# The mixer's output projection by seven products per pair of output tiles, part of them beside the delta rule

## The chip, the core and the metric

The kernel runs on one core of one Trainium2 chip. The metric is device time in microseconds (us); the figure that is compared is the median of several executions, and one further execution was profiled. TensorE (PE) multiplies, VectorE (DVE) and ScalarE (ACT) split operands and move results, GpSimd (POOL) does a few elementwise steps and issues the transfers that add into their destination, SyncE (SP) issues most loads. Transfers of all queues run on the same 16 DMA engines.

## The reference, cut to what matters

One layer of an encoder trunk on 512 tokens of width 2048. The change concerns the end of the mixer and one piece of the cross-attention:

```python
o = gated_delta_rule(q, k, v, g, beta)              # 8 heads x 128 channels, chunks in sequence
y_gdn = rmsnorm(o, out_gain) * silu(z)               # 1024 channels, "heads"
y_sc  = b_gate * causal_dwconv(c_gate * h, conv_w)   # 1024 channels, "convolution"
x = x + concatenate([y_gdn, y_sc], -1) @ w_mix_out   # 2048 x 2048: the output projection
...
v = (mem_n @ w_v)                                    # 256 memory tokens, 4 heads x 512
o = einsum('bhsm,bmhd->bshd', softmax(s), v)
x = x + o @ w_o                                      # w_o = w_xo
```

The kernel never forms `o @ w_o`: it multiplies each head's values by that head's rows of `w_xo` once (the *fold*) and applies the probabilities to the product.

## The kernel before

Everything is fp32, and accuracy is kept by splitting an operand into a high part, rounded to the matmul's format, and a low part, the difference: one ACT cast and one DVE subtraction. In the *three-product form* (`mm3`, L154) a weight block costs three matmuls of 512 columns per 128 channels: high weights by high and by low activations, low weights by high ones. In the *two-product form* (`mm2s`, L168) the activations of half the tokens (256) lie with their high and low parts side by side in one 512-column operand `xo`, so a block costs a matmul of 512 columns with the high weights and one of 256 columns with the low ones.

The stages, in order of time:

- *Values and fold* (to about 193 us). The values of the four heads; then 16 steps (L669 on), a head's quarter of the output columns each: two blocks of `w_xo`, 24 matmuls of 512 columns, results `psmo` scaled into `mo` and stored in `mo_d`. Beside it the operands of the input projection are prepared (`up_prepare`).
- *Input projection* (to 738 us): 28 pairs of output tiles, each by Strassen's scheme in the form with seven products of half size instead of eight, in the two-product form. Sums of weight blocks come partly from DMAs that add into their destination (L544, L550, issued by POOL), partly from DVE.
- *Keys, and queries folded into keys* (738 to 969 us). From here on the delta rule is woven in: generators issue its small steps, and `tick`, called after each planned piece of PE work with that piece's cost, decides when the next step's instructions are issued.
- *Output projection, first half* (from 969 us): `out_row` (L1076) for 16 output tiles, the eight convolution blocks each, 24 matmuls in the three-product form; tile plus `x` goes to `xp_d` in HBM. It is what PE does while the delta rule waits between its steps. *Second half* (to 1177 us): the heads' results `y_d` are loaded (L1074), split, and 16 tiles of 24 matmuls follow; `xp_d` is added, the row stored in `x1_d`, squared for the norm, and split into the operands of the next stage.
- *Scores* (`pss`, 1177 to 1268 us): four sweeps of 96 matmuls, each over the 16 tiles of `x1` against `wk_d`. Then the attention's output and the feed-forward network.

PE's order is the program's in stretches marked `manual_schedule`, and a list scheduler's elsewhere; each engine then runs its list strictly in order, and an instruction waits for the data it needs. The lists of SP and POOL are in order too, so a DMA issue that waits holds back all behind it. Weight blocks are staged in five buffers (`wst`), sums in four (`us`).

## Time and profile before

| | us |
|---|---|
| three runs | 2658.38, 2660.89, 2663.46 (median 2660.89) |
| the profiled execution | 2657.3 (its span, first to last instruction: 2655.5) |
| output projection in the profile, `psx` L156 to L158 | 968.9 to 1177.0 |
| the fold, `psmo` | 99.9 to 193.0 |
| scores, `pss` L1187 to L1189 | 1177.2 to 1267.7 |
| PE busy over the span | 2641.0 |
| granted TensorE clock | 0.999 |

Rows of stretches name the window and then, for each engine, busy time with the number of instructions, the granted clock, the mean busy share of the 16 DMA engines (packets can overlap, so it may pass 1) and the rate of what they moved. In groups, `out<-in` are the program's tile names.

### The profile page before, as it was taken

What the parts mean: (1) busy time and instruction counts of PE and PEld (TensorE: products, weight loads), DVE (VectorE), ACT (ScalarE), POOL (GpSimd) and SP (SyncE); (2) the same over time, 40 slices, a digit from 0 to 9 for tenths busy, and PEclk for the clock granted to TensorE, in tenths of its full rate; (3) what the DMA queues carried; (4) which work ended last, traced back from release to release, by engine and by line L of the source; (5) the groups of instructions that cost most, each with busy time, mean ns of one, the idle gap of its engine ahead of it and who ended that gap; (6) DMA issues with size and microseconds to landing.
All of it is one profiled execution on the core that took longest, in us unless ns stands there. A gap on an engine that the chain in (4) does not pass through costs nothing.

```text
span 2655.5 us, 40192 instructions
## 1 busy us (share of the span) xinstructions
PE 2641.0 (99%) x14759; PEld 2287.8 (86%) x14759; DVE 2251.5 (85%) x3357; ACT 1568.8 (59%) x2283; POOL 234.5 (9%) x280
## 2 busy tenths in 40 slices
PE   9999999999999999999999999999999999999998
PEld 8878888888889998888888888888888888888886
DVE  7878888999988774556789999999999999877888
ACT  7675555665665674445666565655656565554445
POOL 0000000000110022100000000000000000000202
PEclk9999999999999999999999999999999999999999
DMA  8786666777777885765556777777676776864987
GB/s 303 231 276 182 185 158 172 202 191 192 193 220 245 279 262 172 231 199 188 175 160 178 199 178 197 173 193 192 171 196 180 189 187 209 262 186 143 274 269 186
DMA packets 256693, 542.86 MB, mean 204 GB/s; under 512 B 28000, under 2 KB 118256, under 8 KB 256496
## 3 DMA queue, kind: packets, MB, share of 16 engines
q1 hardware_dynamic: 180848, 392.91, 45.8%
q0 software_dynamic: 30816, 95.45, 20.5%
q10 hardware_dynamic: 44832, 51.94, 5.5%
q8 instruction: 116, 1.90, 0.3%
q14 instruction: 81, 0.66, 0.1%
HBM read 471.78 MB, written 67.39 MB: 203 GB/s over the span
## 4 chain that ended last, share of the span: by engine, by line
PE 96%; DVE 1%; ACT 1%; DMA 1%; issue 0%; SPq 0%; DVEq 0%; ACTq 0%
PE px L174 30%; PE pz L174 15%; PE py L174 7%; PE psd L1539 5%; PE psd L1535 5%; PE psd L1536 5%; PE psx L156 3%; PE psx L157 3%; PE psx L158 3%; PE psk L174 3%; PE psk L1091 2%; PE pswk L1110 1%; PE pswk L1118 1%; PE pswk L1112 1%; PE psk L1094 1%; PE pss L1187 1%
## 5 line engine op out<-in xcount | busy, mean ns | idle before, releaser
L174 PE MATMUL px<-xo,whi 128*128 128x512 f32 x2288 | 564.5, 391 | 1.0 <-ACT ga L593 1.0
L174 PEld LDWEIGHTS px<-xo,whi 128*128 128x128 f32 x2288 | 420.1, 188 | 83.6 <-ACT ga L593 2.4
L531 ACT CAST whi<-wst 128x1024 fp32r<-128x1024 f32 x290 | 305.1, 1053 | 239.3 <-PE pz L174 116.9
L532 DVE TENSOR_TENSOR wlo<-wst,whi 128x1024 fp32r<-128x1024 f32 x290 | 353.1, 1219 | 43.2 <-ACT whi L531 42.3
L146 DVE TENSOR_TENSOR wlo<-wst,whi 128x1024 fp32r<-128x1024 f32 x204 | 249.8, 1231 | 83.9 <-ACT whi L145 81.5
L174 PE MATMUL px<-xo,wlo 128*128 128x256 f32 x2288 | 314.9, 283 | 0.9 <-DVE wlo L532 0.9
L174 PEld LDWEIGHTS px<-xo,wlo 128*128 128x128 f32 x2288 | 301.1, 191 | 13.1 <-DVE wlo L532 1.6
L145 ACT CAST whi<-wst 128x1024 fp32r<-128x1024 f32 x204 | 212.7, 1050 | 146.2 <-PE psx L157 40.0
L174 PE MATMUL pz<-xo,whi 128*128 128x512 f32 x1152 | 286.9, 391 | 0.6 <-ACT whi L531 0.6
L532 DVE TENSOR_TENSOR wlo<-s,whi 128x1024 fp32r<-128x1024 f32 x214 | 260.5, 1218 | 5.3 <-ACT whi L531 5.0
L531 ACT CAST whi<-s 128x1024 fp32r<-128x1024 f32 x214 | 223.5, 1048 | 44.6 <-PE px L174 28.6
L174 PEld LDWEIGHTS pz<-xo,whi 128*128 128x128 f32 x1152 | 211.7, 188 | 41.6 <-ACT whi L531 0.8
L1535 PE MATMUL psd<-whi,hdh 128*128 128x512 f32 x616 | 239.7, 389 | 0.0
L1536 PE MATMUL psd<-whi,hdl 128*128 128x512 f32 x616 | 239.6, 389 | 0.0
L1539 PE MATMUL psd<-wlo,hdh 128*128 128x512 f32 x616 | 169.4, 390 | 0.5 <-DVE wlo L1329 0.5
L1326 ACT CAST whi<-wst 128x1024 fp32r<-128x1024 f32 x96 | 101.2, 1054 | 106.6 <-issue 49.6
L174 PE MATMUL pz<-xo,wlo 128*128 128x256 f32 x1152 | 161.2, 283 | 0.0
L174 PEld LDWEIGHTS pz<-xo,wlo 128*128 128x128 f32 x1152 | 152.9, 191 | 5.6
L174 PE MATMUL py<-xo,whi 128*128 128x512 f32 x560 | 139.4, 391 | 0.0
L1539 PEld LDWEIGHTS psd<-wlo,hdh 128*128 128x128 f32 x616 | 115.5, 188 | 25.6 <-DVE wlo L1329 1.7
L1536 PEld LDWEIGHTS psd<-whi,hdl 128*128 128x128 f32 x616 | 115.6, 188 | 24.1
L1535 PEld LDWEIGHTS psd<-whi,hdh 128*128 128x128 f32 x616 | 115.7, 188 | 24.0
(375 smaller groups left out, 4937.3 us busy)
## 6 DMA issues: line engine op xcount, KB each, us to landing
wst<-in_w_up SPq DMA_DIRECT2D x132, 512.0 KB, 4.7
wst<-in_w_dn SPq DMA_DIRECT2D x118, 512.0 KB, 4.5
s<-in_w_up POOLq DMA_DIRECT2D x87, 512.0 KB, 6.2
wst<-in_w_mix SPq DMA_DIRECT2D x84, 512.0 KB, 5.3
s<-in_w_mix POOLq DMA_DIRECT2D x55, 512.0 KB, 6.2
s<-in_w_up SPq DMA_DIRECT2D x43, 512.0 KB, 4.5
hid<-hf_d SPq DMA_DIRECT2D x77, 256.0 KB, 5.3
wst<-in_w_xo SPq DMA_DIRECT2D x32, 512.0 KB, 5.1
```

The lines of the kernel that those rows point to most:

```text
L145: nc.scalar.copy(hi, st)
L146: nc.vector.tensor_tensor(lo, st, f(hi), op=ALU.subtract)
L156: nc.tensor.matmul(ps, wh, xh, start=first, stop=False)
L157: nc.tensor.matmul(ps, wh, xl, start=False, stop=False)
L158: nc.tensor.matmul(ps, wl, xh, start=False, stop=last)
L174: nc.tensor.matmul(dst, w[:, k * P : (k + 1) * P], x[:, :n] if low else x, start=opens, stop=closes, skip_group_check=True)
L531: nc.scalar.copy(hi, t)
L532: tt(lo, t, f(hi), op=ALU.subtract)
L1326: nc.scalar.copy(hi[:, i * n : (i + 1) * n], t)
L1535: nc.tensor.matmul(bs[b], xs[0][:, c], w[0][:, n], start=first, stop=False)
L1536: nc.tensor.matmul(bs[b], xs[1][:, c], w[0][:, n], start=False, stop=False)
L1539: nc.tensor.matmul(bs[b], xs[0][:, c], w[1][:, n], start=False, stop=last)
```

## The change

The output projection becomes eight pairs of output tiles (n, n+8), each by seven half-size products in the two-product form. Write c for the convolution channels' and h for the heads' operand, LO and HI for the token halves. Per pair, three products need little or nothing of the last delta-rule chunks: `m1` (w[n,1] by c LO), `m5` (w[n+8,1]+w[n+8,0] by c HI minus c LO) and `m2` (w[n,0] by h LO). They run beside the delta rule as *jobs*, together with the fold of the fourth head, taken out of the earlier fold stage; that head's values travel through HBM (`vt_d`) to get there. m1 and m1+m5 are parked in `q_d`, the weight sum of m5 in `s1_d`.

The other four products (operands 6, 3, 7, 4) follow when the delta rule is done, in a *second loop* over the eight pairs. For each pair SP loads three blocks of `w_mo`, the parked sum and a fourth block; ACT negates the first block; POOL issues two DMAs that add it into the other two (`s2`, `s3`). A finished row is completed by two more adding DMAs (`x`, then the parked `q_d`), stored in `x1_d`, squared, and the square added into one of two sums by another adding DMA. `x1_d`'s consumers now take tiles in pairs (n, n+8).

```diff
-    folds = [(hd, ng, q) for hd in range(XH) for ng in range(4) for q in range(2)]
+    LATE = XH - 1
+    folds = [(hd, ng, q) for hd in range(LATE) for ng in range(4) for q in range(2)]
...
-        for step in range(4 * XH):
+        for step in range(4 * LATE):
...
+    jobs = [("fold", ng, q) for ng in range(4) for q in range(2)] + [("m1", 0, 0)]
+    for n in range(HK):
+        jobs += ([("m1", n + 1, 0)] if n + 1 < HK else []) + [("m5", n, 0)]
+    jobs += [("m2", n, 0) for n in range(HK)]
...
+        elif kind == "m5":
+            nc.sync.dma_start(t, g["w_mo"][HK + n, 1])
+            nc.gpsimd.dma_start(t, g["w_mo"][HK + n, 0], accum_op=ALU.add)
...
+    def filled(ps, w, r, first):
+        for kk in range(HK):
+            nc.tensor.matmul(ps, w[0][:, kk * P : (kk + 1) * P], xop[r][kk], start=first and kk == 0, stop=False, skip_group_check=True)
+            place(0.23)
+        for kk in range(HK):
+            nc.tensor.matmul(ps[:, HI], w[1][:, kk * P : (kk + 1) * P], xop[r][kk][:, LO], start=False, stop=kk == HK - 1, skip_group_check=True)
+            place(0.12)
...
-    def out_row(n, xs):
-        ps = PM("psx1")
-        hi, lo = piece()
-        for k in range(8):
-            mm3(ps, hi[:, k * P : (k + 1) * P], lo[:, k * P : (k + 1) * P], *xs[k], k == 0, k == 7)
-            place(0.69)
-        return ps
...
-        ps = out_row(n, yp)
-        x0 = T("x0r")
-        nc.sync.dma_start(x0, xp_d[n])
-        nc.vector.tensor_tensor(x0, ps, x0, op=ALU.add)
-        nc.sync.dma_start(x1_d[n], x0)
-        add_squares(acc1, x0, n == 0)
-        x1p.append(split(x0, "x1"))
...
+    def post_load(n):
+        if n >= HK or n in raws:
+            return
+        a11, a22, a12 = raw(g["w_mo"][n, 1]), raw(g["w_mo"][HK + n, 0]), raw(g["w_mo"][n, 0])
+        raws[n] = a22, a12
+        nc.scalar.activation(a11, a11, AF.Identity, scale=-1.0)
+        s2s[n], s3s[n] = US("s2"), US("s3")
+        for t, src in ((s2s[n], s1_d[n]), (s3s[n], g["w_mo"][HK + n, 1])):
+            nc.sync.dma_start(t, src)
+            nc.gpsimd.dma_start(t, a11, accum_op=ALU.add)
...
+    def row_done(n, t):
+        nc.gpsimd.dma_start(t, g["x"][n], accum_op=ALU.add)
+        nc.gpsimd.dma_start(t, q_d[n % HK], accum_op=ALU.add)
+        nc.sync.dma_start(x1_d[n], t)
+        late_x1.append((n, t))
+
+    def row_parts():
...
+            sq = T("sq")
+            nc.scalar.activation(sq, t, AF.Square)
+            nc.gpsimd.dma_start(acc, sq, accum_op=ALU.add)
+        x1p[n] = split(t, "x1")
...
+        for n in range(HK):
+            a22, a12 = raws[n]
+            w6 = wsplit(s2s[n])
+            px = PG("px")
+            mm2s(px, *w6, xop[6], True, True)
+            tt(a12, a12, s2s[n], op=ALU.subtract)
+            gb = T("gb")
+            nc.scalar.copy(gb, px)
+            w3 = wsplit(a12)
+            post_load(n + 1)
+            if fourth:
+                fourth()
+            pz = PG("pz")
+            mm2s(pz, *w3, xop[3], True, True)
+            w7 = wsplit(s3s[n])
+            mm2s(px, *w7, xop[7], False, True)
```

Three places show how the lists of the engines change. The first is POOL's list from the end of the delta rule on. Before, POOL loads the heads' results (`yg`) and then has nothing until the feed-forward network's weights (`w_up`):

```order
L1058 TENSOR_TENSOR so_11138<-so_11138,z_11247 128x512
L1059 DMA y_d<-so_11138 128x4x128
L1074 DMA yg_11361<-y_d 128x512
L1074 DMA yg_11367<-y_d 128x512
L1074 DMA yg_11373<-y_d 128x512
L1074 DMA yg_11379<-y_d 128x512
L1074 DMA yg_11385<-y_d 128x512
L544 DMA s_2507_13715<-in_w_up 128x1024
```

Now it issues the second loop's adding DMAs there; this is the piece from the third pair's weight sums on (`s2`, `s3` of 128x1024; `x1` is a row):

```order
L1234 DMA s2_2112_11758<-wst_2109_11751 128x1024
L1234 DMA s3_2113_11759<-wst_2109_11751 128x1024
L1296 DMA x1_2021_11317<-in_x 128x512
L1297 DMA x1_2021_11317<-q_d_86 128x512
L1234 DMA s2_2129_11869<-wst_2126_11862 128x1024
L1296 DMA x1_2102_11720<-in_x 128x512
L1234 DMA s3_2130_11870<-wst_2126_11862 128x1024
L1296 DMA x1_2032_11365<-in_x 128x512
L1297 DMA x1_2102_11720<-q_d_86 128x512
L1297 DMA x1_2032_11365<-q_d_86 128x512
L1234 DMA s2_2150_11990<-wst_2147_11983 128x1024
```

Rows' and weights' additions stand in one list, and both additions of a row name the same tile. The end of that piece, from the eighth pair's last weight sum on:

```order
L1234 DMA s3_2220_12366<-wst_2216_12358 128x1024
L1296 DMA x1_2071_11547<-in_x 128x512
L1297 DMA x1_2180_12188<-q_d_86 128x512
L1309 DMA acc1macc_11633<-sq_2204_12316 128x512
L1297 DMA x1_2071_11547<-q_d_86 128x512
L1309 DMA acc1xacc_11634<-sq_2207_12323 128x512
L1296 DMA x1_2203_12313<-in_x 128x512
L1297 DMA x1_2203_12313<-q_d_86 128x512
L1296 DMA x1_2079_11586<-in_x 128x512
L1297 DMA x1_2079_11586<-q_d_86 128x512
L1296 DMA x1_2226_12438<-in_x 128x512
L1297 DMA x1_2226_12438<-q_d_86 128x512
```

Behind the last weight sum stand 13 additions to rows and 10 of squares. The third place is POOL's list beside the delta rule, where before only the delta rule's own steps (`s1`, `qd`, `so`) and stores stood:

```order
L1099 DMA wst_1910_10732<-in_w_mo 128x1024
L996 TENSOR_TENSOR qd_1916_10759<-gb_1804_10230,q_1867_10524 128x512
L1099 DMA wst_1925_10816<-in_w_mo 128x1024
L1099 DMA wst_1938_10888<-in_w_mo 128x1024
L1045 TENSOR_TENSOR s1_1928_10829<-s1_1928_10829,q_1820_10311 128x512
L1099 DMA wst_1949_10950<-in_w_mo 128x1024
L1099 DMA wst_1965_11049<-in_w_mo 128x1024
L1045 TENSOR_TENSOR s1_1956_10996<-s1_1956_10996,q_1838_10391 128x512
```

Each delta-rule step on POOL now stands behind additions of `w_mo`, each of which waits for its own load.

More of the change, by code (lines that the diff above doesn't have):

```diff
@@ L473, in trunk @@
         vts = values(g["w_xv"], fold_pieces, beside_values)
+    for i in range(XD // P):
+        nc.gpsimd.dma_start(vt_d[i], vts[LATE * 4 + i])
     ident = mk[:, M_ID, :]
@@ L697, in trunk @@
                     nc.tensor.matmul(pss[mt], v_[:, mt * P : (mt + 1) * P], lo[:, wsl], start=False, stop=kk == 3)
-            if step == 4 * XH - 1:
+            if step == 4 * LATE - 1:
                 begin_parts(first)
@@ L1065, in trunk @@
     order += [g["w_xq"][i, q] for i, q in turns]
-    order += [g["w_mo"][n, 1] for n in range(KT)]
     for hb in range(2):
@@ new lines, in job_split @@
+    def job_split(i):
+        if i < len(jobs) and i not in jparts:
+            job_load(i)
+            jparts[i] = wsplit(jraw[i])
+            if jobs[i][0] == "m5":
+                nc.scalar.dma_start(s1_d[jobs[i][1]], jraw[i])
+    def filled(ps, w, r, first):
[5 more added lines that the diff above has]
+            place(0.12)
@@ new lines, in halves_sum, with fold_late @@
+    def halves_sum(dst, ps):
+        nc.scalar.copy(dst, ps[:, HI])
+        tt(dst, ps[:, LO], dst, op=ALU.add)
+    def fold_late(ng, q, w):
+        if q == 0:
+            jps["fold"] = [PM("psmo") for _ in range(2)]
+        hi, lo = w
+        for mt in range(2):
+            ps = jps["fold"][mt]
+            for low in range(2):
+                for kk in range(2):
+                    v_, wsl = vlate[2 * q + kk], slice(kk * S, (kk + 1) * S)
+                    for part in range(1 if low else 2):
+                        c = part * NMEM + mt * P
+                        nc.tensor.matmul(ps, v_[:, c : c + P], (lo if low else hi)[:, wsl], start=q == kk == low == part == 0, stop=q == kk == low == 1)
+                        place(0.23)
+            if q:
+                t = T("mo")
+                nc.scalar.activation(t, ps, AF.Identity, scale=rmc[:, mt : mt + 1])
+                nc.scalar.dma_start(mo_d[2 * LATE + mt][:, ng * S : (ng + 1) * S], t)
@@ new lines, in conv_ready, with heads_load, heads_low, heads_high @@
+    def conv_ready(n):
+        a = ya[n]
+        xop[1].append(beside(a[:, LO]))
+        tt(a[:, LO], a[:, HI], a[:, LO], op=ALU.subtract)
+        xop[5].append(beside(a[:, LO]))
+    def heads_load(h0, halves_):
+        for h in range(h0, h0 + 4):
+            if len(yb) == h:
+                yb.append(T("yg"))
+            for sl in halves_:
+                nc.gpsimd.dma_start(yb[h][:, sl], y_d[h][:, sl])
+    def heads_low(h):
+        xop[2].append(beside(yb[h][:, LO]))
+    def heads_high(h):
+        a, b = ya[h], yb[h]
+        tt(a[:, LO], b[:, HI], a[:, LO], op=ALU.subtract)
+        xop[6].append(beside(a[:, LO]))
+        xop[3].append(beside(b[:, HI]))
@@ L1122, in trunk, with ask @@
         nc.scalar.dma_start(wk_d[i][:, q * S : (q + 1) * S], wk)
-    for n in range(KT):
-        ps = out_row(n, yp)
-        x0 = T("x0r")
-        nc.sync.dma_start(x0, g["x"][n])
-        nc.vector.tensor_tensor(x0, ps, x0, op=ALU.add)
-        nc.sync.dma_start(xp_d[n], x0)
+    for n in range(4):
+        vlate.append(T("kth", F32R))
+        nc.gpsimd.dma_start(vlate[n], vt_d[n])
+    todo = []
+    asked = set()
+    def ask(what, needs, then):
+        if what not in asked and needs <= stored:
+            asked.add(what)
+            todo.extend(then)
@@ L1130, in trunk @@
     while chains:
         tick(1.0)
-    dstack.close()
-    order += [g["w_mo"][n, 0] for n in range(KT)]
-    yp = [split(loaded(y_d[h], nc.gpsimd), "yp") for h in range(H)]
-    acc1 = cpool.tile([P, S], F32, tag="macc", name="acc1")
-    x1p = []
-    for n in range(KT):
-        ps = out_row(n, yp)
-        x0 = T("x0r")
-        nc.sync.dma_start(x0, xp_d[n])
-        nc.vector.tensor_tensor(x0, ps, x0, op=ALU.add)
-        nc.sync.dma_start(x1_d[n], x0)
-        add_squares(acc1, x0, n == 0)
-        x1p.append(split(x0, "x1"))
+    if not opened:
+        dstack.close()
+        open_pool(uss, "us", 4, reuse_waits="tile")
@@ new lines, in trunk, with fourth @@
+    with tc.manual_schedule(engines={mybir.EngineType.PE}):
+        fourth = None
+        for n in range(HK):
[14 more added lines that the diff above has]
+            mm2s(px, *w7, xop[7], False, True)
+            tt(gb, pz, gb, op=ALU.add)
+            tt(rows[n][:, HI], gb[:, LO], gb[:, HI], op=ALU.add)
+            row_done(n, rows[n])
+            rb = T("x1")
+            halves_sum(rb[:, HI], px)
+            def fourth(n=n, px=px, rb=rb, a22=a22):
+                mm2s(px, *wsplit(a22), xop[4], False, True)
+                halves_sum(rb[:, LO], px)
+                row_done(HK + n, rb)
+            if 1 < n < 6:
+                row_parts()
+                row_parts()
+        fourth()
```

119 lines of the change are left out of this document (103 added, 16 removed).

## Prediction, made before the result was known

> **What bounds the kernel now.** I read the page first, its busy times and the chain of work that ended last, then stretches of time around the output projection.
>
> ```profile
> span 2655.5 us, 40192 instructions
> PE 2641.0 (99%) x14759; PEld 2287.8 (86%) x14759; DVE 2251.5 (85%) x3357; ACT 1568.8 (59%) x2283; POOL 234.5 (9%) x280
> PE 96%; DVE 1%; ACT 1%; DMA 1%; issue 0%; SPq 0%; DVEq 0%; ACTq 0%
> ...
> 968.70:1090.00 121.30, 121.30 (x807) 102.27 (x806) 61.50 (x92) 62.33 (x86) 35.37 (x33) 1.00 0.64 208
> 1090.00:1177.20 87.20, 87.20 (x386) 72.22 (x385) 51.64 (x65) 34.95 (x49) 0.00 (x0) 1.00 0.64 202
> 1177.20:1200.00 22.80, 22.80 (x106) 19.03 (x105) 12.59 (x14) 10.29 (x11) 0.00 (x0) 1.00 0.59 196
> ```
>
> PE sets the time: 2641 of 2655.5 us, 96% of the chain, and in the output projection (first half with the delta rule, second half, first sweep of the scores) it never rests. So a matmul less is time gained, and any wait the change brings to PE is time lost. The last two numbers of the stretches are the ones to keep: the DMA engines are busy for 0.64 and 0.59 of the time. This change moves far more bytes than it removes matmuls.
>
> **PE's part.** The group rows of the second half, a matmul of the old form:
>
> ```profile
> L157 PE MATMUL psx<-ypl,whi 128*128 128x512 f32 x129 | 50.0, 389 | 0.0
> L158 PE MATMUL psx<-yph,wlo 128*128 128x512 f32 x129 | 50.0, 389 | 0.0
> L156 PE MATMUL psx<-yph,whi 128*128 128x512 f32 x128 | 49.6, 389 | 0.0
> ```
>
> 128 + 129 + 129 = 386 in 87.2 us are 0.226 us each (the 389 ns overlap). Both halves are 2 x 16 x 24 = 768 such matmuls: 173.5 us. The new form already runs in the input projection; this is PE there, with ends left out:
>
> ```profile
> 421.29 2.00 PE L174 MATMUL px<-xo,whi 128*128 128x512 f32 x8
> ...
> 426.86 3.82 PE L174 MATMUL px<-xo,whi 128*128 128x512 f32 x16
> ...
> 432.43 2.00 PE L174 MATMUL py<-xo,whi 128*128 128x512 f32 x8
> ```
>
> From 421.29 to 432.43 lie exactly four products (32 matmuls of each width): 11.14 us, 2.785 each. The change needs 8 pairs x 7 = 56: 156.0 us. **PE saves 173.5 - 156.0 = 17.5 us.** The fold of the fourth head keeps its 96 matmuls; it leaves a stage where PE, DVE and ACT have 70 and 76 of 93 us to do,
>
> ```profile
> 99.90:193.00 93.10, 93.03 (x422) 72.96 (x422) 70.12 (x128) 75.80 (x131) 1.71 (x2) 1.00 0.82 258
> L146 DVE TENSOR_TENSOR wlo<-wst,whi 128x1024 fp32r<-128x1024 f32 x30 | 35.6, 1221 | 14.0 <-ACT whi L145 13.9
> L145 ACT CAST whi<-wst 128x1024 fp32r<-128x1024 f32 x30 | 30.3, 1048 | 6.5 <-PE psk L174 2.6 <-PE psmo L695 1.8 <-ACT mo L702 1.6
> L702 ACT ACTIVATE mo<-psmo,rmc 128x512 f32<-128x512 f32 x30 | 18.9, 682 | 6.2 <-PE psmo L697 6.2
> ```
>
> and takes 8 x 1.22 = 10 us of DVE and 8 x 1.05 + 8 x 0.68 = 14 us of ACT along, so about 60 and 62 of 71 us stay: still covered, 0 us. In the second loop a pair costs DVE about 9.5 us (five 1.22 passes, the rest short) and ACT about 9 us against PE's 11.1: also covered, if the data come.
>
> **The DMA engines' part.** I price transfers in units of 512 KB. A plain copy, when the queues are full, and an adding copy (POOL's), alone, on average, and when its queue is full:
>
> ```profile
> 1069.00:1077.00 8.00, 8.00 (x37) 6.63 (x36) 2.03 (x3) 4.65 (x6) 0.30 (x1) 1.00 1.02 373
> 413.11 0.86 POOL L550 DMA_DIRECT2D s<-in_w_mix  x1 [9.12 <-ACT s L549]
> 413.00:418.50 5.50, 5.50 (x34) 4.85 (x33) 4.52 (x6) 3.53 (x6) 0.86 (x1) 1.00 0.59 98
> 2592.00:2622.00 30.00, 30.00 (x134) 24.84 (x133) 28.60 (x48) 21.74 (x45) 15.73 (x19) 1.00 1.08 219
> q0 software_dynamic: 2514, 4.60, 86.0%
> q1 hardware_dynamic: 1537, 1.93, 21.8%
> ```
>
> Copies alone: 373 GB/s, 1.41 us a unit. One adding unit, issued at 413.11, fills the next window alone: 0.59 x 5.5 = 3.24 us of all engines. From 2592 to 2622 POOL adds without pause; 4.60 MB by q0 beside 1.93 MB by q1 (5.2 us at 373 GB/s) leave 24.8 us for 8.77 units: 2.83 us. The input projection as a whole (300 to 700 us) gives the upper prices:
>
> ```profile
> q1 hardware_dynamic: 12203, 43.96, 33.7%
> q0 software_dynamic: 5936, 21.51, 32.1%
> ```
>
> 134.8 us for 83.8 units, 1.61 us; 128.4 us for 41.0 units, 3.13 us. That adding from one on-chip tile to another is no cheaper, three 256 KB squares show (60 to 95 us): 0.80 MB, 4.8 us, 3.1 us a unit.
>
> ```profile
> q0 software_dynamic: 442, 0.80, 13.6%
> macc<-sq POOLq DMA_DIRECT2D x3, 256.0 KB, 5.3
> ```
>
> A pair of the second loop moves five plain units of weights, one of stored rows, two adding units of weights, two of rows (four of 256 KB) and one of squares: 6 x 1.41 + 5 x 2.83 = **22.6 us** (25.3 at the upper prices) **against 11.1 us of PE**. Five `wst` and four `us` buffers let little be fetched ahead. So the second loop is bound by the DMA engines, and I follow POOL's list to find when PE gets its last weights:
>
> - *Beside the delta rule.* 32 weight loads, 8 adding units, 8 units of parked sums, 4 of `q_d`, 4 of `mo_d`, 2 of values and 4 of `yg` (at the plain price), and some 20 us of the delta rule's own traffic (0.64 x 121.3 = 78 us, less the 41 plain units of `w_mo`, five of them for the second half, `x`, `xp_d` and `yg`): 54 x 1.41 + 8 x 2.83 + 20 = 119 us (132 at the upper prices) for PE's 121. Just covered; I add **8 us** (0 to 19) for the heads' results, which `m2` waits for.
> - *Second loop to its last weight sum.* Ahead of it in the list are all 16 weight sums, 9 rows, one more `x` and 4 squares: 16 + 11.5 adding units, with 44.5 plain ones: 140.5 us. Four loads come early (5.6 us), buffers allow four products' lead (11 us); cast, difference and two products follow (8 us): 132 us; twice a row's second addition stands right behind its first and stops POOL for some 4 us (the 5.3 us landing above, less an issue): 140 against 32 x 2.785 = 89. **+51 us** (43 without those stops; 68 at the upper prices).
> - *Into the scores.* 13 row additions and 10 squares stand behind that sum: 11.5 units, 33 us, with 10 plain units 47 us, and the last row must land and be split (3 us) before the first sweep's end. PE has two products and seven eighths of a 22.8 us sweep, 28 us. **+22 us, +5** for the last squares, which the norm's matmuls wait for (15 to 35).
>
> Sum against the profiled execution: 2657.3 - 17.5 + 8 + 51 + 27 = **2725.8 us**; it lies 3.6 below the median of the runs, so **2729 us**. With all lower bounds 2701, with all upper ones 2765. The granted clock is 1.00 in every stretch above, where PE never waits; with waits it need not stay. [...]
>
> **Rivals.** *(A) Adding costs no more than copying once requests queue, and the loop stays on PE: faster.* For it: a lone adding unit lands 6.2 us after issue, a plain one 5.3,
>
> ```profile
> s<-in_w_mix POOLq DMA_DIRECT2D x41, 512.0 KB, 6.2
> wst<-in_w_mix SPq DMA_DIRECT2D x63, 512.0 KB, 5.3
> ```
>
> little apart. Against it: the full queue at 2592 to 2622. At 1.41 us for both kinds the list to the last weight sum is 72 x 1.41 - 5.6 - 11 + 8 = 93 us, +4, the scores wait perhaps 2: 2657.3 - 17.5 + 6 + 3.6 = 2649. [...] *(B) The delta rule is slowed as well.* Its steps on POOL stand behind additions that wait for loads. Now:
>
> ```profile
> 1059.54 1.28 POOL L1040 TENSOR_TENSOR s<-s,q 128x512 f32<-128x512 f32 x1 [8.93 <-ACT s L1037]
> 1077.66 1.67 POOL L1058 TENSOR_TENSOR so<-so,z 128x512 f32<-128x512 f32 x1 [8.37 <-DVE so L1056]
> 1082.97 2.13 POOL L1074 DMA_DIRECT2D yg<-y_d  x4 [2.01 <-DMA y_d<-so]
> ```
>
> POOL is free when each is due, yet from `s` (1059.54) to the results back on chip (1085.1, and 5 more to land) are some 30 us, of which PE's list covers about 24 from the norm's matmul on. If six additions each delay a step by a landing (6.2 us), 37 us come on top: 2766. *(C) Rows are finished later than I count and the scores, at 0.59 DMA share, swallow them:* only the second loop's 51 us stand, and the 8 and 27 around it fall away: 2729 - 8 - 27 = 2694. *(D) No rest at all on PE*, the pure count of matmuls: 2643; 2 in 100, with A.
>
> **Chances.** The forecast (2705 to 2750) 0.55, B (2750 to 2800) 0.19, C (2670 to 2705) 0.17, A and D 0.09. What a measurement can tell from no change is about 0.2%, 5.3 us: 2655.6 to 2666.2. A and D fall mostly below that band, C's lower end hardly reaches it: faster 0.07, same 0.03, slower 0.90. Leaving out A, D and the tail of B, the range is 2680 to 2780.
>
> **What would show it.** In the second loop PE's pair takes about 17 to 20 us instead of 11.1; PE's waits there go through `whi` and `wlo` to `s` and so to a DMA; the DMA share is near 1.1 at 220 to 260 GB/s; POOL's row additions wait for the DMA before them. The first sweep of the scores waits for `x1h`. PE's busy time falls by some 17 us. I am wrong if the loop runs at 11 to 13 us a pair with the DMA share under 0.9, or if most lost time lies before 1090 us.

## The result: 4.4% slower, and the profile after

The changed kernel takes **2778.75 us** (median; 2776.67 to 2784.49), beside it the kernel before 2662.16 us (2658.38 to 2663.46): a ratio of **1.0444** (95% interval 1.0424 to 1.0463), 116.6 us more. The forecast was 2729 (2705 to 2750). The page of the changed kernel, its busy times and its granted clock over 40 slices:

```profile
span 2776.4 us, 40951 instructions
PE 2662.9 (96%) x14895; PEld 2306.4 (83%) x14895; DVE 2302.3 (83%) x3470; ACT 1621.8 (58%) x2403; POOL 301.9 (11%) x362
...
PEclk9999999999999999887999999999999999999999
```

PE was busy for 2641.0 of 2655.5 us; now it rests 113.5 us instead of 14.5. And although it has 17.5 us less to do, it is busy 21.9 us *longer*: 2662.9 - (2641.0 - 17.5) = 39.4 us, put down here to a lower granted clock, which is lowest in slices 17 to 19 (0.8, 0.8, 0.7). The stretches of the changed kernel, in the columns of the front part (PE, PEld, DVE, ACT, POOL, granted clock, DMA share, GB/s): queries, products beside the delta rule, second loop, scores.

```profile
823.20:954.80 131.60, 128.38 (x1219) 125.86 (x1218) 108.03 (x241) 85.52 (x148) 17.57 (x23) 1.00 0.85 273
954.80:1131.03 176.23, 141.26 (x907) 119.07 (x906) 98.00 (x168) 98.45 (x164) 49.04 (x53) 0.87 0.84 245
1131.03:1272.70 141.67, 99.24 (x493) 84.04 (x492) 67.97 (x90) 56.22 (x85) 37.51 (x43) 0.86 0.99 252
1272.70:1389.55 116.85, 101.43 (x443) 82.31 (x442) 62.02 (x98) 56.72 (x103) 13.08 (x15) 0.91 0.76 202
```

Set beside the forecast's own stages: the second loop takes 141.7 us (forecast 140), the scores 116.9 (forecast 90.5 + 27 = 117.5). But the second loop *begins* at 1131.0. The forecast's beginning is 968.7, less the fold's 21.7 that left the front, plus 88.5 for 24 products and the fold, plus 34.6 for the delta rule's own matmuls (121.3 less half of 173.5), plus 8: 1078.1. That is 52.9 us, and the whole miss is 52.4 (2778.2 against 2725.8 in the profiled executions): it lies before the second loop. Set against the delta rule's steps, 3.6 us of the loss come before the first of the copies named below, 44.5 between the first and the last, and 12.8 behind the last, of which the forecast had 8.

What PE waits for in the second loop, and how the transfers fare there (waits: us in total, times, longest; queues: packets, MB, share of 16 engines; issues: count, size, median us to landing):

```profile
PE px L176 <- DVE wlo L537: 28.5, 5, 10.8
PE px L176 <- DVE x L1120: 11.9, 4, 6.4
```

```profile
q0 software_dynamic: 6197, 14.45, 55.6%
q1 hardware_dynamic: 7133, 21.22, 42.7%
...
wst<-in_w_mo SPq DMA_DIRECT2D x18, 512.0 KB, 8.6
s<-wst POOLq DMA_DIRECT2D x12, 512.0 KB, 8.2
```

The adding queue q0 moves fewer bytes than the plain q1 and takes more of the engines. Both kinds of unit land in over 8 us, where 5.3 and 6.2 were usual in the input projection.

Now the stage that went wrong. The delta rule's output is copied eight times (`so`, L1038 before, L1043 after). From the first copy to the last, before and after:

```profile
931.40:1061.40 130.00, 130.00 (x996) 115.51 (x995) 77.23 (x126) 76.96 (x110) 32.38 (x26) 1.00 0.69 216
```

```profile
913.30:1087.80 174.50, 146.01 (x1050) 128.59 (x1049) 99.75 (x172) 98.63 (x155) 45.91 (x46) 0.89 0.82 248
```

PE's list holds the same work between these copies in both kernels: weighted by its columns (an estimate at 0.226 us for 512, the rate of the second half before: 386 matmuls in 87.2 us) it comes to 106.2 us before and 106.4 after. By the clock it is the same too: 146.0 x 0.89 = 129.9. So of the **44.5 us** that this stretch grew, 16.0 are clock and 28.5 are waits. The waits are many and small, and most end with a step of DVE, 6.8 us of them with a late load of the fourth head's values:

```profile
PE pso L1026 <- DVE vn L1017: 9.1, 3, 5.9
PE psmo L1133 <- DMA kth<-vt_d: 6.8, 2, 4.9
PE pr L853 <- DVE st L1031: 3.6, 1, 3.6
PE psq L1112 <- DVE q L1120: 2.6, 1, 2.6
PE pv L853 <- DVE v L1012: 2.3, 1, 2.3
PE psa L857 <- DVE pt L957: 2.2, 1, 2.2
```

The longest of them, on DVE and PE in order of time (start, duration, instruction, idle time before it):

```profile
1071.13 1.22 DVE L537 TENSOR_TENSOR wlo<-wst,whi 128x1024 fp32r<-128x1024 f32 x1
1076.79 0.43 DVE L1158 TENSOR_TENSOR yg<-yg,yg 128x256 f32<-128x256 f32 x1 [4.44 <-DMA yg<-y_d]
...
1080.87 0.69 DVE L1017 TENSOR_TENSOR vn<-pv,bk 128x512 f32<-128x512 f32 x1
```

```profile
1081.61 0.80 PE L1026 MATMUL pso<-dt,vn 128*128 128x128 f32 x2 [5.88 <-DVE vn L1017]
```

`vn` is a step of the delta rule, and its product `pv` was done. But in DVE's list a difference of the first heads' results (`yg`) stands ahead of it, and waits for a load. Behind that come eight more steps, none of which `vn` needs, then `vn`, and PE rests 5.88 us. The load was one of those that POOL issued from 1069.30 on. They took 7.0 to 10.4 us to land (5.2 in the median before), while from 1069 to 1077 us the DMA engines were busy for 0.99 of the time:

```profile
1069.30 4.13 POOL L1151 DMA_DIRECT2D yg<-y_d  x7
1069.00:1077.00 8.00, 6.73 (x43) 5.88 (x41) 2.85 (x8) 1.53 (x3) 4.98 (x9) 1.00 0.99 280
```

SP's list has the same order of things. Its weight loads wait for a free buffer (38.1 us in the longest group of these waits), and the delta rule's own loads stand behind them: POOL waited 30.2 us for loads of `z`, against 5.2 before, and the last two went out at 1101.4, 13.6 us after the last copy of `so` began (4.8 before). What that alone cost PE is not measured.

### The profile page after: what moved, and what is told of

It reads as the page before. It is cut to its first block, busy times and chain, and to the rows that moved or that the text cites. A ratio compares the mean times of both kernels' runs of the same rounds, so it can differ in the third digit from the quotient of the medians.

```text
span 2776.4 us, 40951 instructions
## 1 busy us (share of the span) xinstructions
PE 2662.9 (96%) x14895; PEld 2306.4 (83%) x14895; DVE 2302.3 (83%) x3470; ACT 1621.8 (58%) x2403; POOL 301.9 (11%) x362
## 4 chain that ended last, share of the span: by engine, by line
PE 50%; DVE 1%; ACT 0%; DMA 0%; issue 0%; DVEq 0%; ACTq 0%
PE px L176 17%; PE pz L176 9%; PE psd L1743 5%; PE psd L1739 5%; PE psd L1740 5%; PE py L176 4%; PE psx L160 1%; PE psx L158 1%; PE psx L159 1%; PE pss L1392 1%; PE pss L1393 1%; PE pss L1391 1%; DMA wst<-in_w_dn 0%; DVE wlo L1533 0%; PE psxt L1448 0%
## 5 line engine op out<-in xcount | busy, mean ns | idle before, releaser
L176 PE MATMUL px<-xo,whi 128*128 128x512 f32 x2480 | 620.3, 395 | 22.7 <-DVE x L1120 11.9
L176 PEld LDWEIGHTS px<-xo,whi 128*128 128x128 f32 x2480 | 458.9, 190 | 114.1 <-DVE x L1120 12.7
L537 DVE TENSOR_TENSOR wlo<-wst,whi 128x1024 fp32r<-128x1024 f32 x338 | 415.7, 1232 | 74.5 <-ACT whi L536 71.6
L176 PE MATMUL px<-xo,wlo 128*128 128x256 f32 x2480 | 346.6, 286 | 29.5 <-DVE wlo L537 29.4
L176 PEld LDWEIGHTS px<-xo,wlo 128*128 128x128 f32 x2480 | 331.2, 194 | 46.0 <-DVE wlo L537 32.8
L176 PE MATMUL pz<-xo,whi 128*128 128x512 f32 x1216 | 303.8, 392 | 0.6 <-ACT whi L536 0.6
L537 DVE TENSOR_TENSOR wlo<-s,whi 128x1024 fp32r<-128x1024 f32 x230 | 279.9, 1219 | 7.3 <-ACT whi L536 7.0
L536 ACT CAST whi<-s 128x1024 fp32r<-128x1024 f32 x230 | 240.0, 1047 | 76.5 <-PE px L176 35.4
L176 PEld LDWEIGHTS pz<-xo,whi 128*128 128x128 f32 x1216 | 224.2, 189 | 43.7 <-ACT whi L536 0.8
L148 DVE TENSOR_TENSOR wlo<-wst,whi 128x1024 fp32r<-128x1024 f32 x164 | 199.4, 1221 | 56.8 <-ACT whi L147 54.0
L147 ACT CAST whi<-wst 128x1024 fp32r<-128x1024 f32 x164 | 170.9, 1049 | 105.6 <-PE pss L1393 26.3
L176 PE MATMUL pz<-xo,wlo 128*128 128x256 f32 x1216 | 170.2, 283 | 0.0
```

What stands on the lines that cost most here:

```text
L147: nc.scalar.copy(hi, st)
L148: nc.vector.tensor_tensor(lo, st, f(hi), op=ALU.subtract)
L176: nc.tensor.matmul(dst, w[:, k * P : (k + 1) * P], x[:, :n] if low else x, start=opens, stop=closes, skip_group_check=True)
L536: nc.scalar.copy(hi, t)
L537: tt(lo, t, f(hi), op=ALU.subtract)
```

## Experiments

Each changed one thing in the changed kernel, unless said otherwise. Times are medians, ratios are against the kernel before on the same chip in the same job (it measured 2658.9 to 2660.0 there). Theory 1 and theory 2 are named anew in each expectation. The stages are those of one profiled execution each: wst6, us5, store_after and lists, equal as wholes, differ by 8.6 us in the loop and by 5.9 in the stretch, so a few us in one stage alone say little. The measured stages of all runs (the stretch is that from the first to the last copy of `so`):

| run | us | ratio (95%) | stretch | beside delta rule | second loop | scores |
|---|---|---|---|---|---|---|
| the change | 2778.8 | 1.0444 (1.0424-1.0463) | 174.5 | 176.4 | 141.7 | 116.8 |
| rows_dve | 2742.4 | 1.0305 (1.0289-1.0322) | 176.1 | 176.7 | 121.6 | 99.3 |
| weights_dve | 2761.3 | 1.0382 (1.0361-1.0404) | 173.7 | 172.8 | 128.2 | 114.0 |
| m5_dve | 2770.9 | 1.0414 (1.0399-1.0430) | 166.5 | 162.0 | 142.6 | 118.1 |
| all_dve | 2716.9 | 1.0215 (1.0200-1.0230) | 164.8 | 162.8 | 112.0 | 95.7 |
| best | 2725.7 | 1.0247 (1.0231-1.0262) | 162.4 | 161.4 | 126.5 | 94.7 |
| warm6 | 2813.0 | 1.0572 (1.0554-1.0589) | 174.7 | 178.1 | 183.2 | 108.8 |
| sq_dve | 2767.4 | 1.0405 (1.0389-1.0420) | 172.5 | 174.8 | 138.3 | 108.7 |
| store_after | 2778.3 | 1.0443 (1.0428-1.0459) | 173.0 | 175.5 | 137.3 | 118.2 |
| wst6 | 2779.1 | 1.0440 (1.0423-1.0458) | 177.1 | 179.3 | 143.0 | 117.6 |
| us5 | 2776.9 | 1.0442 (1.0427-1.0458) | 173.4 | 174.5 | 137.8 | 116.5 |
| lists | 2779.0 | 1.0451 (1.0433-1.0468) | 171.2 | 173.8 | 145.9 | 114.8 |
| defer_q | 2783.5 | 1.0456 (1.0439-1.0472) | 176.1 | 178.4 | 131.9 | 127.4 |
| fold_early | 2787.6 | 1.0479 (1.0464-1.0495) | 168.7 | 136.5 | 160.5 | 122.5 |
| kth_sp | 2774.3 | 1.0433 (1.0417-1.0449) | 166.5 | 168.5 | 143.4 | 115.0 |
| job_noload | 2765.9 | 1.0403 (1.0388-1.0419) | 157.0 | 153.1 | 142.6 | 114.8 |
| job_nocast | 2777.1 | 1.0440 (1.0422-1.0457) | 176.2 | 173.5 | 138.1 | 117.7 |
| job_bare | 2758.2 | 1.0369 (1.0353-1.0384) | 155.8 | 149.1 | 134.5 | 117.4 |
| noload_kth | 2756.6 | 1.0358 (1.0341-1.0375) | 153.1 | 148.4 | 140.4 | 120.0 |

### The second loop and the scores: additions off the DMA engines

**rows_dve**: the rows' sums by plain loads and DVE, the squares' sums by DVE.

```diff
-        nc.gpsimd.dma_start(t, g["x"][n], accum_op=ALU.add)
-        nc.gpsimd.dma_start(t, q_d[n % HK], accum_op=ALU.add)
+        for src in (g["x"][n], q_d[n % HK]):
+            xr = T("xr")
+            nc.sync.dma_start(xr, src)
+            tt(t, t, xr, op=ALU.add)
...
-            nc.gpsimd.dma_start(acc, sq, accum_op=ALU.add)
+            tt(acc, acc, sq, op=ALU.add)
```

> Only the finishing of rows is changed: x and the parked sum come by plain loads and DVE adds them, DVE also adds the squares (in all 23 adding units fewer, 16 plain units more). Theory 1 (adding transfers fill the DMA engines, 2.83 us a unit against 1.41): a pair of the second loop falls from 22.6 to 16.9 us of DMA, the loop from 142 to about 112 us, the four score sweeps from 117 to about 95; about 2725 us in all. Theory 2 (the loop waits because each load's latency is not hidden by the few weight buffers, whatever the rows do): loop within 8 us of 142, only the scores gain; about 2760 us.

The loop fell by 20.1 us and the scores by 17.5, the whole by 36.3: two thirds of what theory 1 expected, and far from theory 2, which left the loop where it was.

**weights_dve**: the second loop's weight sums by DVE, from the same loads.

```diff
-        nc.scalar.activation(a11, a11, AF.Identity, scale=-1.0)
...
-            nc.gpsimd.dma_start(t, a11, accum_op=ALU.add)
+            tt(t, t, a11, op=ALU.subtract)
```

> Only the two weight sums of the second loop are changed: plain load, then a DVE subtraction, no negation on ACT (16 adding units fewer, rows still add by DMA). Theory 1: 17.0 instead of 22.6 us of DMA a pair, loop about 118 us, scores unchanged at 117 since the rows' additions still stand one behind the other; about 2755 us. Theory 2 (latency of the load, add, cast chain): one landing of about 6 us less per pair, up to 45 us: about 2735 us. DVE has 12 us a pair to do then, above PE's 11.1, so no less than 96 us for the loop in either.

The loop fell by 13.5 us, the whole by 17.4: less than the price of twelve adding units (34 us), and less than either theory had it (118 us for the loop by theory 1, 2735 us for the whole by theory 2).

**m5_dve**: the sums for `m5`, beside the delta rule, by a second plain load and DVE.

```diff
-            nc.gpsimd.dma_start(t, g["w_mo"][HK + n, 0], accum_op=ALU.add)
+            m5b[n] = [T("m5b") for _ in range(2)]
+            for j, sl in enumerate((slice(0, S), slice(S, 2 * S))):
+                nc.sync.dma_start(m5b[n][j], g["w_mo"][HK + n, 0][:, sl])
...
+                    tt(jraw[i][:, sl], jraw[i][:, sl], t2, op=ALU.add)
```

> Only the eight weight sums beside the delta rule are changed: both blocks by plain loads, DVE adds them; POOL's list holds no addition there any more. Rival B (the delta rule's steps stand behind these additions on POOL): the stage from the end of the queries (965 us) to the second loop (1131 us), 166 us, falls by 30 to 45 us; about 2740 us. Theory 1 alone (throughput): 8 units at 1.42 us less each, some 11 us; 2767 us. If the stage is slow because of TensorE's clock and DVE's and ACT's own waits: within 8 us of 2779 us.

The stage beside the delta rule fell by 14.4 us, the stretch in it by 8.0, the whole by 7.8. The price of the transfers alone was to give some 11 us of the stage. So what the prediction's rival B (POOL's steps of the delta rule delayed behind additions) adds can't be told apart from that price, and the two together are worth 14 us here, not 37.

**all_dve**: the three edits together.

> All additions by DMA in the two places (m5 sums, second loop's weight sums, rows' sums, squares' sums) become plain loads and DVE additions or subtractions. Each alone gave 7.8, 17.4 and 36.3 us. Theory 1 (price of the adding transfers): the gains add up, 61 us: loop at 105 to 112 us (DVE then has about 105 us of work in it), jobs at 160 to 163 us, scores at 99 us, the whole at 2712 to 2722 us, still slower than before, because the jobs beside the delta rule keep 40 us. Theory 2 (circle of waits and lists): DVE becomes the link, the gains do not add up: loop at 118 to 125 us, the whole at 2725 to 2740 us.

2716.9 us: the gains add up (36.3 + 17.4 + 7.8 = 61.5 us of 2778.8 would be 2717.3). The second loop and the scores in this run:

```profile
1117.83:1229.80 111.97, 92.06 (x491) 78.34 (x490) 105.90 (x144) 53.77 (x81) 0.00 (x0) 0.94 0.79 269
1229.80:1325.45 95.65, 95.31 (x443) 78.62 (x442) 69.30 (x112) 56.81 (x103) 0.00 (x0) 1.00 0.65 200
```

The scores are back at full clock and nearly at their old length. The adding transfers are all gone here, and 57 us over the kernel before remain; PE rests for 20 us in this loop and for 26 beside the delta rule (137.2 busy of 162.8 there).

**best**: as all_dve, but the second loop's weight sums on POOL, and the fourth head's values loaded on SP.

```diff
-            tt(t, t, a11, op=ALU.subtract)
+            nc.gpsimd.tensor_tensor(t, t, a11, op=ALU.subtract)
...
-        nc.gpsimd.dma_start(vlate[n], vt_d[n])
+        nc.sync.dma_start(f(vlate[n]), f(vt_d[n]))
```

> All additions off the DMA engines as in the run that gave 2716.9 us, but the second loop's weight sums on POOL, which does nothing there (about 2.6 us each, 42 us), instead of DVE, and the fourth head's values loaded on SP. Theory 1 (in that run DVE with 106 of 112 us set the loop): the loop falls to 95 to 103 us, the jobs by 3 to 8 us, the whole to 2695 to 2708 us, still above the kernel before, since 35 to 45 us beside the delta rule remain. Theory 2 (the loop is set by landing times and buffers, not by DVE): the loop stays at 108 to 115 us, the whole at 2710 to 2720 us.

The name was wrong: the loop got 14.5 us longer than in all_dve, beyond both theories. POOL's sum takes 2.66 us where DVE's takes about 1.22, and its list waits for the loads:

```profile
L1238 POOL TENSOR_TENSOR s<-s,wst 128x1024 f32<-128x1024 f32 x12 | 31.8, 2661 | 77.2 <-DMA s<-s_d 47.9 <-DMA wst<-in_w_mo 10.8 <-DVE wlo L537 9.5
```

With a DMA share of 0.67, PE busy for 98.7 and DVE for 107.7 of 126.5 us nothing is full here. I read it so that without adding transfers the loop is set by how long a weight takes from its load through the sum and the cast to PE; no further run tests that. No run beat the kernel before.

**sq_dve**: only the fourteen additions of squares go to DVE (the last line of rows_dve's edit).

> Only the fourteen additions of squares to the two sums of squares go to DVE instead of adding transfers; no product, weight or row waits for them inside the second loop. At the 1.41 us that such a half unit costs in an adding transfer they are 20 us of DMA time. Theory 1 (the DMA engines are the shared resource that sets the loop's pace, so any transfer taken away from them pays): loop and scores together, 258.5 us, fall by 14 to 20 us, the whole to 2758 to 2765 us. Theory 2 (a circle of waits through the weights' and rows' own steps, where transfers beside it do not count): loop and scores fall by less than 6 us, the whole stays at 2772 to 2780 us.

Loop and scores together fell by 11.6 us, the whole by 11.4: nearer to theory 1, short of its range. The DMA engines' busy time over both stages (share times length) went from 0.99 x 141.7 + 0.76 x 116.8 = 229.1 us to 0.97 x 138.3 + 0.69 x 108.7 = 209.1: the 20 us off that fourteen half units at 2.83 us a unit make. Done the same way for the other runs, a microsecond of DMA time taken away shortened the two stages by 0.53 us (weights_dve, 30.8 us taken), 0.58 (sq_dve), 0.65 (all_dve, 78.5) and 0.82 (rows_dve, 46.1).

### The second loop: is it the engines, or buffers and lists?

**warm6** adds six unused matmuls of 512 columns ahead of each of the loop's 32 products, 43 us of PE work.

```diff
+    def keep2(c=6):
+        for _ in range(c):
+            nc.tensor.matmul(v4(warm2), onesr, onesr.unsqueeze(1).broadcast_to([P, 4, P]), start=True, stop=True)
```

> Six matmuls of 512 columns that nothing uses, put before each of the 32 products of the second loop (32 x 6 x 0.2265 = 43 us of PE work at full clock), which keep TensorE from resting as long. If DMA sets the loop's pace: within 8 us of 2779 us, and the granted clock in the loop rises from about 0.87 to above 0.95. If the halved clock after each wait is what makes the loop long: up to 12 us shorter, 2767 us. If PE's own work set the pace: 43 us longer, 2822 us.

The loop grew by 41.5 us (loop and scores together by 33.5) and its clock stayed at 0.86. Were the DMA engines alone the limit, the added work would have been hidden. So theory 1 was in doubt, and the five runs after this one test a circle of waits instead. What PE waited for in this loop, and the landings:

```profile
PE px L176 <- DVE x L1120: 36.6, 5, 8.9
PE px L176 <- DVE wlo L537: 2.0, 1, 2.0
...
wst<-in_w_mo SPq DMA_DIRECT2D x18, 512.0 KB, 4.1
s<-wst POOLq DMA_DIRECT2D x12, 512.0 KB, 6.4
```

PE hardly waits for weights any more, and landings fall from 8.6 and 8.2 to 4.1 and 6.4 us: the engines are less crowded (share 0.87). PE waits for the halves' sum (`x`, L1120) instead. DVE, which makes it, stands longest at a weight difference that waits for its block; but it stood there about as long in the changed kernel (second view):

```profile
DVE wst L1326 <- DMA wst<-in_w_mo: 59.4, 6, 13.2
```

```profile
DVE wst L1319 <- DMA wst<-in_w_mo: 55.9, 6, 16.5
```

So this wait in DVE's list is part of the loop with crowded engines and without. That the lists, and no longer the engines, set the loop once PE has more to do is a reading of these waits, not a finding.

**store_after** puts the sixteen stores of finished rows on SP behind the last weight load. **wst6** has six weight buffers, **us5** five buffers for the sums (each paid with two of 66 small tiles). **lists** is store_after and us5 together.

```diff
-        nc.sync.dma_start(x1_d[n], t)
+        stores.append((n, t))
...
+    with tc.issue_after(lastld[0].ins):
+        while stores:
+            m, t = stores.pop(0)
+            nc.sync.dma_start(x1_d[m], t)
```

```diff
-WST = 5
+WST = 6
```

```diff
-            open_pool(uss, "us", 4, reuse_waits="tile")
+            open_pool(uss, "us", 5, reuse_waits="tile")
```

> The sixteen stores of the finished rows (x1_d) are put on SP behind the last of the second loop's weight loads; not one transfer, byte or buffer is changed. In the changed kernel SP stood 106 us at these stores, waiting for the rows' additions, with weight loads queued behind them. Theory 1 (the DMA engines are full in the second loop, share 0.99, and their bytes and additions set its 141.7 us): the loop stays at 138 to 144 us, the whole at 2775 to 2782 us. Theory 2 (the loop is a circle of waits through a few buffers, and SP's list with the stores in it is a link of that circle): the weight loads go out as soon as their buffers are free, the loop falls to 115 to 128 us, the whole to 2752 to 2765 us.

> One more weight buffer (six instead of five of 128x1024), paid with two of the 66 small 128x512 tiles; nothing else is changed. Theory 2 (few buffers, circle of waits): a load can be one job further ahead, the jobs beside the delta rule fall from 176 us to 160 to 170 us, the second loop from 141.7 to 125 to 135 us, the whole to 2755 to 2770 us. Theory 1 (throughput of the DMA engines in the loop; in-order lists beside the delta rule): the loop stays at 138 to 144 us and the whole at 2772 to 2782 us.

> Five instead of four buffers for the second loop's weight sums, paid with two of the 66 small tiles, so that the next but one pair's first sum can start before this pair's second is cast. Theory 1 (DMA engines full, their bytes and additions set the pace): the loop stays at 138 to 144 us. Theory 2 (circle: free buffer, load of 8 us, addition of 9 us, cast, free buffer): the loop falls to 122 to 132 us and the whole to 2760 to 2770 us.

> Two changes at once that each alone gave 4 us of the loop: five buffers for the weight sums, and the rows' stores behind the last weight load on SP. Theory 1 (DMA engines): the loop stays at 134 to 140 us. Theory 2 (several links of about equal length close the circle, so that opening one shows nothing): together they give much more than their sum, the loop falls to 115 to 128 us.

Loops of 137.3, 143.0, 137.8 and 145.9 us, the whole between 2776.9 and 2779.1: all four go against the circle as far as these links go. Neither store order nor a buffer more, nor two of these links at once, is worth anything that can be measured.

**defer_q** issues each row's second addition a pair later, behind the next weight sums' additions, and stores as in store_after.

> The rows' second addition (q_d) is issued a pair later, behind the next weight sums' additions on POOL, when the first addition has long landed; the rows' stores stand behind the last weight load on SP. The same transfers, bytes and additions. In the changed kernel POOL waited 107 us of the second loop's 141.7 (55.2 us of it at the second additions, for the first to land) and issued for 37.5: its list was never free. Theory 1 (DMA engines full, share 0.99): the loop stays at 134 to 142 us. Theory 2 (POOL's in-order list is the circle: product, row, first addition, its landing, second addition, and only then the next weight sum's addition, cast and product; this also fits that added matmuls lengthened the loop by their whole time): the loop falls to 100 to 122 us, the whole to 2740 to 2765 us, the scores keep what the late additions leave them.

Of 55.2 us that POOL waited in the loop for the first additions to land, 14.0 are left. But POOL's list was hardly freer: it waited 71.3 us ahead of the weight sums for a copy on ACT and a difference on DVE, where it had waited 28.4, and 101 us in all, against 107. The loop fell by 9.8 us only, and the scores took 10.6 more. POOL's waits and the landings of the row additions in this loop:

```profile
POOL s L1234 <- ACT x L1119: 38.9, 4, 13.9
POOL s L1234 <- DVE wlo L537: 32.4, 3, 16.4
POOL x L1242 <- DMA x<-in_x: 14.0, 2, 8.9
```

```profile
x<-in_x POOLq DMA_DIRECT2D x13, 256.0 KB, 10.5
x<-q_d POOLq DMA_DIRECT2D x12, 256.0 KB, 12.3
```

The second additions landed in 12.3 us instead of 6.7 (the first in 10.5 instead of 8.9). The waits changed place, in POOL's list and in the transfers' queue, and the DMA share stayed at 0.98. That fits the DMA engines as the limit of this loop; warm6 shows that they are not its only one.

### Beside the delta rule

**fold_early** folds the fourth head in the fold stage, as before; the seven products stay.

```diff
-    LATE = XH - 1
+    LATE = XH
...
-    jobs = [("fold", ng, q) for ng in range(4) for q in range(2)] + [("m1", 0, 0)]
+    jobs = [("m1", 0, 0)]
```

> The fourth head's values are folded in the fold stage as in the kernel before, so no fold jobs stand beside the delta rule; the seven products stay as they are. Theory 1 (beside the delta rule the new work is stalled by late loads of values and weights at its start): the stage before the keys takes 17.8 us more, the jobs fall from 176 to 125 to 132 us, the whole to 2743 to 2752 us. Theory 2 (the delta rule's own steps, slowed by transfers and casts in the same lists, set that stage, and the fold runs in its gaps): the jobs fall by no more than 15 to 25 us, the whole stays at 2770 to 2782 us.

The whole got 8.9 us slower, which neither theory had. The jobs fell by 39.9 us, but the stage up to the keys took its 22.1 back, and the second loop grew by 18.8, for it now waits for the delta rule's end. PE's largest wait in that loop:

```profile
PE px L176 <- DVE xo L510: 20.5, 2, 19.7
```

The stretch itself stays at 168.7 us, 5.8 less than in the changed kernel. So the fold is not what lengthens the delta rule: its steps arrive late with the fold beside them and without.

**job_noload** leaves out the weight loads of 24 jobs, **job_nocast** the casts, **job_bare** both, and **noload_kth** is job_noload with the fourth head's values on SP; **kth_sp** changes these values' loads alone.

```diff
         kind, n, q = jobs[i]
+        if i:
+            jraw[i] = jraw[0]
+            return
```

```diff
-            jparts[i] = wsplit(jraw[i])
+            jparts[i] = jparts[0] if i else wsplit(jraw[i])
```

> Leaves out the weight loads of the 24 jobs after the first beside the delta rule (and with them the m5 additions by DMA): every job casts the first job's resident tile again. Casts, products and all steps of the delta rule stay. Measured so far from the first to the last copy of the delta rule's output (so, L1038 before, L1043 after): 130.0 us before with PE never idle, 174.5 us after with the same PE work, 28.5 us of it PE idle and 16 us from a clock of 0.89. Theory 1 (late weights: casts that wait for transfers stand in ACT's and DVE's lists ahead of the delta rule's steps): the stretch falls to 138 to 150 us and the jobs' stage from 176 to 140 to 152 us, as in the run without casts. Theory 2 (the casts themselves, twice as many per us of PE work as before, crowd ACT and DVE): the stretch stays at 160 to 172 us.

> Leaves out the 24 casts and splits of the jobs' weights after the first (every job multiplies by the first job's halves); the weight loads and the m5 additions stay, but nothing on ACT and DVE waits for them. Theory 1 (late weights): the stretch from the first to the last copy of so comes to 138 to 150 us, no better than in the run that leaves out the loads. Theory 2 (the casts crowd ACT and DVE): here alone it falls to 132 to 145 us, 20 us or more below the run without loads. The late load of the fourth head's values (6.8 us) stays in both.

> Beside the delta rule neither weights are loaded nor cast for the 24 jobs after the first (each multiplies by the first job's halves); the delta rule, the products, the halves' sums, the stores and the preparation of the heads' operands stay. Without the loads alone the stretch from the first to the last copy of so was 157.0 us, before 130.0 us. Theory 1 (the rest is still the weights' path, the casts in the lists of ACT and DVE): the stretch falls to 130 to 140 us. Theory 2 (the rest are the other new steps in these lists: the halves' sums that wait for a product's end, and the heads' operands that wait for stores and loads): it stays at 148 to 158 us.

> The four late loads of the fourth head's values go out on SP instead of POOL, where they stood behind the delta rule's output step (so, y_d). Theory 1 (this wait of 6.8 us is one of several independent waits, and it is what first halves the clock): the fold jobs are 7 us shorter and the first stretch runs at full clock, the whole falls by 7 to 18 us, to 2760 to 2772 us. Theory 2 (the delta rule's own chain sets the stage, waits only change place): the jobs' stage stays at 172 to 178 us and the whole at 2774 to 2782 us.

> As the run that leaves out the weight loads beside the delta rule, and the fourth head's values loaded on SP. From the first to the last copy of so: 174.5 us in the changed kernel, 157.0 without the loads, 166.5 with the values on SP, 130.0 before. Theory 1 (independent waits in front of PE, each with its share of halved clock): 144 to 151 us. Theory 2 (what remains is set by the delta rule's steps and the halves' sums, waits only change place): 153 to 159 us.

The stretch (174.5 us in the changed kernel) came to 157.0, 176.2, 155.8, 166.5 and 153.1 us. Job_nocast's is no clean number: its late values waited longer,

```profile
PE psmo L1133 <- DMA kth<-vt_d: 21.7, 2, 19.9
```

but job_bare against job_noload, 1.2 us, shows that the casts as such cost nothing. The loads, with the additions among them, are worth 17.5 us of the stretch and 12.8 us of the whole, since the stretch also began 4.5 us later; POOL's late value loads 8.0 and 4.4; both together 21.4 and 22.1. That is about half of the 44.5 us. The other 23 remain with no weight load and no late value, 14.4 as waits and 8.7 as clock:

```profile
913.60:1066.70 153.10, 138.67 (x1047) 124.04 (x1047) 99.34 (x170) 100.99 (x158) 35.22 (x34) 0.94 0.51 176
PE pso L1026 <- DVE vn L1017: 6.5, 3, 4.4
PE psa L857 <- DVE pt L957: 3.3, 1, 3.3
PE pswk L1199 <- ACT wk L1210: 2.9, 1, 2.9
```

Nearly all of these waits (13.8 of 14.4 us) end before 975 us, where the last queries and the first jobs meet. The longest of them has the shape seen above, with a load of the delta rule's own (`xd`) in place of the heads' results: DVE stands for it, six more steps follow in its list, then `vn`, and PE rests.

```profile
949.80 0.69 DVE L957 TENSOR_TENSOR pt<-xd,mk 128x512 f32<-128x512 f32 x1 [5.77 <-DMA xd<-xd_d]
...
954.21 0.80 PE L1026 MATMUL pso<-dt,vn 128*128 128x128 f32 x2 [4.40 <-DVE vn L1017]
```

## Why the prediction was wrong, point by point

- **The step that failed** is *Beside the delta rule*: "Just covered; I add **8 us** (0 to 19) for the heads' results". It weighed 119 us of transfers against PE's 121 and took the stage as covered. Measured: the second loop begins 52.9 us later than that step has it, and this is all of the miss. The transfers were undersized: 0.84 of 176.2 us are 148 us of engine time, where the sum had 119 (132 at its upper prices); part of that, four additions among it, is for the second loop. On average they still left room, and yet loads came late, since in pieces they were full (0.99 from 1069 to 1077 us). So what failed besides the size is the form of the argument: sums of busy time do not say whether a step comes in time. The delta rule gives PE a step of 0.8 us of matmuls, then some us of other work, then the next; its DVE and ACT steps now stand in one list with casts, halves' sums and heads' differences that wait for a load or for PE. The same list held casts before, with PE work of one weight block twice as long behind each (24 matmuls at 0.226 us, 5.4 us, against 2.785), and PE never waited. Of the stretch's 44.5 us the loads and late values account for 21, by the run without them. That the remaining 23 come from the order of the other steps in these lists, and from loads of the delta rule's own that come late, is what the waits show one by one (the 5.88 and the 4.40 us above); no run took that order away, so it is argued and not shown.
- **The clock** has no term in the sum; the forecast says only that with waits it need not stay at 1.00. Measured, it was 0.86 in the second loop (PE busy 99.2 us there for 89.1 us of work: 10 us), 0.89 in the delta rule's stretch (16.0 us) and 0.91 in the scores (about 10.9 us, 101.4 against 90.5); in all 39.4 us of busy time are put down to it. It is part of the 52.9 us and, in loop and scores, hidden in sizes that came out right.
- **Second loop, 140 us against 89**: measured 141.7. The signs named came: 17.7 us a pair, waits through `wlo`, 252 GB/s, POOL's second additions waiting for the first. The DMA share was 0.99, not 1.1. Prices held where they could be tested: the squares' 14 half units took 20.0 us, as priced. But that time is a limit on top of waits, not the only one: a microsecond less of DMA gave 0.5 to 0.8 us, and 43 us more PE work cost 33.5. So the size came out right with a mechanism that the runs bear out in part.
- **Into the scores, +27**: measured +26.3, and the waits are those that were told, by another list. PE waited 15.4 us, 14.0 of them in two waits of 7.0 for the cast of a block of the scores' weights. Both casts stood in ACT's list behind the square of a row, which waited for that row's second addition, 4.74 us the first time and 11.24 the second. The other 10.9 us are the clock, which the sum left out; the waits were to be 27. (The 28 us of PE's work in that term are 25.5 by its own parts, two products and seven eighths of 22.8, so it should have read 2.5 us more.) The mechanism held; that the sum fits is partly luck.

```profile
PE pss L1391 <- ACT whi L147: 14.0, 2, 7.0
...
1308.31 0.63 ACT L1308 ACTIVATE sq<-x 128x512 f32<-128x512 f32 x1 [11.24 <-DMA x<-q_d]
...
1309.35 2.94 ACT L147 CAST whi<-wst 128x1024 fp32r<-128x1024 f32 x3
1310.44 0.80 PE L1391 MATMUL pss<-whi,x1h 128*128 128x512 f32 x1 [7.00 <-ACT whi L147]
```

- **PE's 17.5 us**: the saving is there, but the forecast that busy time falls by some 17 us was wrong, since 39.4 came on top. That this is the clock fits the granted clock of the whole run, 0.98: 2623.5 / 2662.9 is 0.985.
- **The rivals.** A (adding costs no more than copying) is refuted by sq_dve and rows_dve, and D (no rest at all on PE) by PE's 113.5 us of rest. B named the right stage and came nearer with its total, 2766, by a mechanism that m5_dve prices at 14 us of that stage at most, instead of 37. C's swallowing by the scores did not come; they got longer. The named sign of error, most lost time before 1090 us, did not quite come either: 61 us ahead of the second loop (8 expected and 53), 53 in it, 26 in the scores.

## What to carry to other kernels

When spare work is put beside a chain of dependent steps, ask of each in-order list what will stand ahead of the chain's steps in it, and what that waits for; a stage whose busy times all fit can still be a third longer. A tenth fewer matmuls in a stage don't pay for transfers that add, where a pair of tiles then needs, by the prices above, 22.6 us of the DMA engines for 11.1 us of PE. Once PE rests in many short waits, count the clock as a term of its own: here 39 of the 138 us lost.

## What the runs showed of the hardware that was not expected

**The granted clock fell from 1.00 to 0.50 soon after PE began to rest, and came back while PE worked without a rest.** From the first waits of the stage beside the delta rule on, in steps of 6 us:

```profile
952.00:958.00 6.00, 4.36 (x49) 4.05 (x47) 4.84 (x11) 5.82 (x11) 0.98 (x1) 1.00 0.14 54
958.00:964.00 6.00, 2.74 (x10) 2.07 (x10) 2.69 (x5) 2.23 (x6) 0.85 (x2) 0.58 0.94 280
964.00:970.00 6.00, 3.69 (x13) 2.40 (x13) 1.10 (x2) 0.00 (x0) 4.22 (x5) 0.50 0.86 241
970.00:976.00 6.00, 2.63 (x6) 2.15 (x7) 0.00 (x0) 0.00 (x0) 1.50 (x3) 0.50 0.74 200
976.00:982.00 6.00, 6.00 (x46) 5.22 (x45) 2.31 (x5) 2.65 (x4) 0.00 (x0) 0.72 0.39 105
982.00:988.00 6.00, 5.67 (x43) 3.94 (x41) 2.31 (x4) 5.89 (x9) 0.00 (x0) 1.00 0.34 109
```

By the fourth row PE has rested for 10.6 of 24 us and runs at 0.50; in the fifth, busy for all 6.00 us, it runs at 0.72, and in the sixth at 1.00. Unused matmuls ahead of each product did not raise the clock of the second loop (warm6, 0.86 with and without): PE still rested there for 38.6 us, against 42.4.

**A wait taken out of one list came back in others.** With 41 us of POOL's waits for a row's first addition gone (defer_q), POOL waited 43 us longer ahead of the weight sums, the landing of 256 KB additions went from 6.7 to 12.3 us, and loop and scores together gained nothing (259.3 us against 258.5).
